# Winograd-row convolution on one core: all inputs loaded as fp32 by SyncE, cast by ScalarE, in ten planned 16-KB buffers

## The chip, the core and the metric

The kernel runs on one core of one Trainium2 chip. The metric is device time in microseconds (us). The profile is of one execution and gives times from the start of its span; TensorE is PE in it, VectorE DVE, ScalarE ACT, GpSimd POOL, SyncE SP.

## What is computed

A 3x3 convolution with padding 1, no bias: 16 images of 64 channels, 64 x 64, to 128 output channels, fp32 in and out.

```python
x_pad = np.pad(x, ((0, 0), (0, 0), (1, 1), (1, 1)), mode='constant')
output[b, co] += weight[co, ci, kh, kw] * x_pad[b, ci, kh:kh+h, kw:kw+w]   # over ci, kh, kw
```

The input is 16.8 MB, the output 33.6 MB.

## The kernel before

**Tiling.** Two images make a pair: 2 x 64 channels fill the 128 partitions, so a pair's input is one tile of 128 x 64 x 64, 16 KB per partition in fp32 (2 MB in all). There are 8 pairs. Each image of a pair has its own output tile `ot`, 128 output channels x 64 x 64 in fp32, again 16 KB per partition, 2 MB. The loop at the end runs over the pairs `p` and, in each, over four blocks `blk` of 16 output rows.

**Arithmetic.** Rows are taken two at a time. With G1 the middle row of the kernel, U is G1 applied to the sum of rows 2j and 2j+1 (tile `ss`). The even output row is U plus A, with A from G2-G1 on row 2j+1 and G0 on row 2j-1; the odd one is U plus Bt, with Bt from G0-G1 on row 2j and G2 on row 2j+2. So a block has three groups of matmuls (L165): U of 6, A of 12, Bt of 12, each over the three kernel columns and the two images, each into two PSUM tiles `acc` of 128 x 512; eight such tiles go round. ScalarE copies U to SBUF (`ut`, L179, four buffers), VectorE adds A and `ut` into the even rows of `ot` (L187) and Bt and `ut` into the odd rows (L190).

**Inputs.** Matmuls read fp16: `xs`, the pair's rows, and `ss`, the sums of rows, made by `sums` (L67) on GpSimd one pair ahead (for pair 0 on VectorE). The fp16 rows come in two ways. Pairs 0, 1 and 2 are loaded in fp32 by SyncE's queue at the start (L43, L45, L47), into buffers of the output pool, and cast to fp16 by the function `cast` (L98): pair 0's in the prologue, pair 1's by ScalarE in the last two blocks of pair 0, pair 2's by ScalarE, one piece of 16 rows in each block of pair 1. Pairs 3 to 7 are loaded by GpSimd's queue with a cast in the DMA (`load`, L58): the DMA reads fp32 from HBM and writes fp16. All five are issued early, since `xs` has eight buffers.

**Stores.** `store` (L123) writes a whole output tile of 2 MB at the end of a pair: image 0's is issued by SyncE, image 1's is put in the list `held` and issued by ScalarE in the first block of the next pair, behind the two copies to `ut`. The last pair is stored in halves of 1 MB. The output pool has seven buffers that go round.

**Order.** `keep` fixes the order of the instructions it wraps on their engine. DMA queue q1 is SyncE's, q10 ScalarE's, q0 GpSimd's; all three are worked by the same 16 DMA engines. DMAs that SyncE and ScalarE issue take their completion semaphores in turn from a set of eight; one that takes a semaphore again waits, on the issuing engine, for the DMA that had it before.

Of the kernel before, what the change touches and what calls it, by code (L numbers as in the profile page):

```python
# [8 lines left out]
F32 = mybir.dt.float32  # L9
F16 = mybir.dt.float16  # L10
# [3 lines left out]
def kernel(  # L14
# [6 lines left out]
    nc = tc.nc  # L21
    B, CI, H, W = x.shape
    CO = weight.shape[0]
    assert H == 64 and W == 64 and CI == 64 and CO == 128 and B % 2 == 0
    NP = B // 2
    RB = 8

    keep = tc.keep_in_program_order
    x_rows = x.rearrange("b c h w -> (b c) h w")
# [2 lines left out]

    const = ctx.enter_context(tc.tile_pool(name="const", bufs=1))
    psum = ctx.enter_context(tc.tile_pool(name="psum", bufs=8, space=bass.MemoryType.PSUM))
    xpool = ctx.enter_context(tc.tile_pool(name="xpool", bufs=8))
    opool = ctx.enter_context(tc.tile_pool(name="opool", bufs=7))
    spool = ctx.enter_context(tc.tile_pool(name="spool", bufs=3))
    upool = ctx.enter_context(tc.tile_pool(name="upool", bufs=4))

    w_raw = const.tile([CO, CI * 9], F32)  # L40
    nc.sync.dma_start(w_raw, w_flat)  # L41
    x0 = opool.tile([128, H, W], F32, tag="ot", name="x0")
    nc.sync.dma_start(x0, x_rows[0:128, :, :])  # L43
    x1 = opool.tile([128, H, W], F32, tag="ot", name="x1")
    nc.sync.dma_start(x1, x_rows[128:256, :, :])  # L45
    x2 = opool.tile([128, H, W], F32, tag="ot", name="x2")
    nc.sync.dma_start(x2, x_rows[256:384, :, :])  # L47
    raws = {1: x1, 2: x2}
    ident = const.tile([128, 128], F16)
    make_identity(nc, ident)  # L50
    w16 = const.tile([CO, CI * 9], F16)
    keep(nc.gpsimd.tensor_copy(w16, w_raw))  # L52

    xs = {p: xpool.tile([128, H, W], F16, tag="xs", name="xs") for p in range(3)}

    def load(p):
        xs[p] = xpool.tile([128, H, W], F16, tag="xs", name="xs")
        keep(nc.gpsimd.dma_start(xs[p], x_rows[128 * p : 128 * p + 128, :, :]))  # L58

    ss = {}  # L60

    def sums(eng, p, src, lo, n):
        if p not in ss:
            ss[p] = spool.tile([128, H // 2, W], F16, tag="ss", name="ss")
        v = src.rearrange("p (j i) c -> p j i c", i=2)
        keep(
            eng.tensor_add(  # L67
                ss[p][:, lo : lo + n, :], v[:, lo : lo + n, 0, :], v[:, lo : lo + n, 1, :]
            )
        )  # L70
# [5 lines left out]
    def wrow(i):  # L76
        return Wt[:, i, :, :].rearrange("p t c -> p (t c)")

    wps = {}
    for kh in (1, 2, 0):  # L80
# [3 lines left out]
            for q in (0, 64):  # L84
                nc.tensor.matmul(wp[q : q + 64, k * CO : k * CO + CO], w16[:, t::9], ident)  # L85
        wps[kh] = wp[:, 0 : 3 * CO]
    blank = const.tile([128, 400], F32)
    keep(nc.vector.memset(blank, 0.0))  # L88
    warm = psum.tile([128, 512], F32, tag="acc", name="warm")
    for _ in range(3):  # L90
# [3 lines left out]
    keep(nc.vector.tensor_sub(wrow(G21), wps[2], wrow(G1)))  # L94
    keep(nc.vector.tensor_sub(wrow(G01), wps[0], wrow(G1)))  # L95

    def cast(copy, p, src, lo, hi):
        keep(copy(xs[p][:, lo:hi, :], src[:, lo:hi, :]))  # L98

    for lo in (RB, 2 * RB, 3 * RB):  # L100
        sums(nc.vector, 0, x0, lo, RB)
    cast(nc.scalar.copy, 0, x0, 0, 18)
    keep(nc.scalar.copy(wrow(G0), wps[0]))  # L103
    keep(nc.scalar.copy(wrow(G2), wps[2]))
    cast(nc.gpsimd.tensor_copy, 0, x0, 34, 50)
    cast(nc.gpsimd.tensor_copy, 0, x0, 50, 64)
    for p in range(3, NP):
        load(p)
    later = {
        (0, 0): [(0, x0, 18, 34)],  # L110
        (0, 2): [(1, x1, 0, 16), (1, x1, 16, 32)],
        (0, 3): [(1, x1, 32, 48), (1, x1, 48, 64)],
    }
    later.update({(1, n): [(2, x2, 16 * n, 16 * n + 16)] for n in range(4)})

    held = []

# [2 lines left out]
    cuts_of = [(whole, whole)] * (NP - 1) + [(halves, halves)]  # L120

    def store(eng, p, b2, ot, lo, hi):
        return eng.dma_start(  # L123
            out_rows[2 * p + b2, :, lo:hi, :],
            ot.rearrange("p j i c -> p (j i) c")[:, lo:hi, :],
        )

    for p in range(NP):
        if p + 1 < NP:
            for lo in (0, 16):  # L130
                sums(nc.gpsimd, p + 1, raws.get(p + 1, xs[p + 1]), lo, 16)
        ots = [
            opool.tile([128, H // 2, 2, W], F32, tag="ot", name="ot") for _ in range(2)
        ]
        for blk in range(4):
            j0 = blk * RB

            def group(wi_rows):

                tiles = [  # L140
                    psum.tile([128, RB, W], F32, tag="acc", name="acc") for _ in range(2)
                ]
                n = 3 * len(wi_rows)
                i = 0
                for wi, off in wi_rows:
                    for kw in (1, 0, 2):
                        c_lo, c_hi = max(0, 1 - kw), min(W, W + 1 - kw)
                        for b2 in range(2):
                            p0 = 64 * b2
                            lo, hi = j0, j0 + RB  # L150
                            if off is None:
                                rhs = ss[p][p0 : p0 + 64, lo:hi, c_lo + kw - 1 : c_hi + kw - 1]
                            else:
                                while 2 * lo + off < 0:
                                    lo += 1
                                while 2 * (hi - 1) + off > H - 1:
                                    hi -= 1
                                first = 2 * lo + off
                                last = 2 * (hi - 1) + off
                                rhs = xs[p][  # L160
                                    p0 : p0 + 64,
                                    first : last + 1 : 2,
                                    c_lo + kw - 1 : c_hi + kw - 1,
                                ]
                            nc.tensor.matmul(  # L165
                                tiles[b2][:, lo - j0 : hi - j0, c_lo:c_hi],
                                Wt[p0 : p0 + 64, wi, kw, :],
                                rhs,
                                start=i == 0,
                                stop=i == n - 1,  # L170
                            )
                        i += 1
                return tiles

            U = group([(G1, None)])
            us = []
            for b2 in range(2):
                ut = upool.tile([128, RB, W], F32, tag="ut", name="ut")
                keep(nc.scalar.copy(ut, U[b2]))  # L179
                us.append(ut)  # L180
            while held:
                keep(store(nc.scalar, *held.pop(0)))
            for piece in later.get((p, blk), ()):
                cast(nc.scalar.copy, *piece)
            A = group([(G21, 1), (G0, -1)])
            for b2 in range(2):
                nc.vector.tensor_add(ots[b2][:, j0 : j0 + RB, 0, :], A[b2], us[b2])  # L187
            Bt = group([(G01, 0), (G2, 2)])
            for b2 in range(2):
                nc.vector.tensor_add(ots[b2][:, j0 : j0 + RB, 1, :], Bt[b2], us[b2])  # L190
            if blk in cuts_of[p][0]:
                store(nc.sync, p, 0, ots[0], *cuts_of[p][0][blk])
            if blk in cuts_of[p][1]:
                held.append((p, 1, ots[1], *cuts_of[p][1][blk]))
    while held:
        keep(store(nc.scalar, *held.pop(0)))

# [29 lines left out]
```

## Time and profile before

| | us |
|---|---|
| time, median of 3 runs | 126.74 (126.69 to 126.74) |
| the profiled execution's own time | 126.52 |
| its span | 124.7 |
| busy: TensorE, VectorE, ScalarE, GpSimd | 107.5, 84.6, 46.6, 37.5 |
| issue to landing: x (fp32, SyncE), xs (casting, GpSimd), 2-MB store by SyncE, by ScalarE | 12.3, 36.1, 20.4, 21.0 (medians) |

The page gives the busy time of each engine, then the span in 40 slices with the busy share in tenths, then the DMA queues, the chain of work that ended last, and the groups of instructions. A queue's line gives its packets, its MB and the time of its packets as a share of 16 engines' span. A line of the table of stretches gives the stretch and its length, then for PE, PEld (weight loads), DVE, ACT and POOL the busy us and the number of instructions, then the granted TensorE clock, the share of the DMA engines and GB/s. Bytes of a DMA are counted as they land, so a casting load counts half of what it reads; the page's HBM line counts what HBM gave and took.

### The profile page before, as it was taken

To read this page: it belongs to the slowest core of one execution; us is meant where nothing else is said; L and a number is where in the kernel's file an instruction comes from. 1 tells how busy PE (TensorE), PEld (TensorE's weight loads), DVE (VectorE), ACT (ScalarE), POOL (GpSimd) and SP (SyncE) were. 2 spreads that over 40 slices of the span, in tenths; PEclk is the share of its full clock that TensorE was granted. 3 is DMA by queue.
4 is the path that set the end of the run, shared out by engine and by line. 5 is a ranking of instruction groups with operands and counts; after the bars stand their busy time and mean duration, and the time that the engine had idled before them with its cause. 6 is when DMAs were issued, how large, how long until landed. Compare 5 with 4: busy or idle time off the path is not lost.

```text
span 124.7 us, 2423 instructions
## 1 busy us (share of the span) xinstructions
PE 107.5 (86%) x984; PEld 50.2 (40%) x984; DVE 84.6 (68%) x135; ACT 46.6 (37%) x78; POOL 37.5 (30%) x28
## 2 busy tenths in 40 slices
PE   0598999999999999999999999999999999991000
PEld 0543444444444444444444444444444444440000
DVE  1009987878877887877777778777877787775000
ACT  4108649966663332433333333333333333330000
POOL 2209992799185001920039000670000000000000
PEclk9999999999999999999999999999999999999855
DMA  5999999999999999999999999999999999999992
GB/s 145 386 436 436 431 310 260 213 168 339 381 339 365 334 381 344 357 368 347 355 360 352 355 381 413 436 436 436 415 426 431 426 426 441 426 407 413 426 418 84
DMA packets 3898, 45.52 MB, mean 365 GB/s; under 512 B 432, under 2 KB 432, under 8 KB 560
## 3 DMA queue, kind: packets, MB, share of 16 engines
q1 hardware_dynamic: 1872, 23.36, 44.9%
q10 hardware_dynamic: 1296, 16.78, 31.8%
q0 software_dynamic: 720, 5.24, 20.8%
q8 instruction: 7, 0.11, 0.3%
q14 instruction: 3, 0.02, 0.0%
HBM read 17.07 MB, written 33.55 MB: 406 GB/s over the span
## 4 chain that ended last, share of the span: by engine, by line
PE 81%; DMA 6%; DVE 2%; issue 1%; DVEq 0%; SPq 0%
PE acc L165 81%; DMA x<-in_x_dram 6%; DVE ot L187 1%; DVE ss L67 1%; DVEq L222 0%; DVE ot L190 0%; SPq L41 0%; DVEq L187 0%
## 5 line engine op out<-in xcount | busy, mean ns | idle before, releaser
L165 PE MATMUL acc<-xs,Wt 64*128 64x504 f16 (+3 forms) x768 | 87.2, 374 | 0.0
L165 PEld LDWEIGHTS <-Wt 64*128 64x128 f16 x960 | 47.4, 95 | 56.2 <-issue 1.2
L179 ACT COPY ut<-acc 128x512 f32<-128x512 f32 x64 | 34.4, 589 | 56.8 <-issue 38.1
L187 DVE TENSOR_TENSOR ot<-acc,ut 128x512 f32<-128x512 f32 x64 | 41.2, 685 | 20.7 <-PE acc L165 18.4
L190 DVE TENSOR_TENSOR ot<-acc,ut 128x512 f32<-128x512 f32 x64 | 41.1, 684 | 0.0
L67 POOL TENSOR_TENSOR ss<-xs 128x1024 f16<-128x1024 f16 x10 | 21.0, 2124 | 34.9 <-DMA xs<-in_x_dram 34.9
L165 PE MATMUL acc<-ss,Wt 64*128 64x504 f16 (+1 forms) x192 | 26.1, 377 | 0.6 <-DVE ss L67 0.6
L98 ACT CAST xs<-x 128x1024 f16<-128x1024 f32 (+1 forms) x10 | 10.5, 1068 | 3.5 <-DMA x<-in_x_dram 3.5
L67 POOL TENSOR_TENSOR ss<-x 128x1024 f16<-128x1024 f32 x4 | 9.4, 2382 | 3.2 <-DMA x<-in_x_dram 3.2
L67 DVE TENSOR_TENSOR ss<-x 128x512 f16<-128x512 f32 x4 | 3.3, 868 | 7.8 <-DMA x<-in_x_dram 7.8
L85 PE MATMUL wp<-ident,w 128*64 128x128 f16 x18 | 1.3, 328 | 4.5 <-POOL w L52 4.5
L98 POOL CAST xs<-x 128x1024 f16<-128x1024 f32 (+1 forms) x2 | 3.0, 1519 | 4.7 <-DMA x<-in_x_dram 4.7
L91 PE MATMUL warm<-blank 128*128 128x400 f32 x6 | 3.5, 738 | 0.0
L85 PEld LDWEIGHTS <-w 128*64 128x64 f16 x18 | 1.1, 209 | 4.5 <-POOL w L52 4.5
L58 POOL DMA_DIRECT2D xs<-in_x_dram x5 | 2.8, 583 | 0.0
L91 PEld LDWEIGHTS warm<-blank 128*128 128x128 f32 x6 | 1.7, 303 | 1.3 <-issue 1.0
L92 ACT CAST Wt<-wp 128x384 f16<-128x384 f32 x1 | 0.5, 478 | 3.1 <-PE wp L85 3.1
L92 ACT ACT_TABLE_LOAD x1 | 1.3, 1283 | 0.7 <-PEq L211 0.7
L52 POOL CAST w<-w_raw 128x576 f16<-128x576 f32 x1 | 0.7, 662 | 2.5 <-DMA w_raw<-in_weight_dram 2.5
L88 DVE MEMSET blank<- 128x400 f32 x1 | 0.4, 392 | 0.9 <-PEq L211 0.9
L103 ACT CAST Wt<-wp 128x384 f16<-128x384 f32 x1 | 0.5, 478 | 0.5 <-DVE Wt L95 0.5
L94 DVE TENSOR_TENSOR Wt<-wp,Wt 128x384 f16<-128x384 f32 x1 | 0.5, 549 | 0.0
(8 smaller groups left out, 1.9 us busy)
## 6 DMA issues: line engine op xcount, KB each, us to landing
out_dram<-ot SPq DMA_DIRECT2D x7, 2048.0 KB, 20.4
out_dram<-ot ACTq DMA_DIRECT2D x7, 2048.0 KB, 21.0
x<-in_x_dram SPq DMA_DIRECT2D x3, 2048.0 KB, 12.3
xs<-in_x_dram POOLq DMA_DIRECT2D x5, 1024.0 KB, 36.1
out_dram<-ot SPq DMA_DIRECT2D x2, 1024.0 KB, 10.7
out_dram<-ot ACTq DMA_DIRECT2D x2, 1024.0 KB, 11.0
w_raw<-in_weight_dram SPq DMA_DIRECT2D x1, 288.0 KB, 3.0
```

What stands on the lines that cost most here:

```text
L52: keep(nc.gpsimd.tensor_copy(w16, w_raw))
L58: keep(nc.gpsimd.dma_start(xs[p], x_rows[128 * p : 128 * p + 128, :, :]))
L67: eng.tensor_add(ss[p][:, lo : lo + n, :], v[:, lo : lo + n, 0, :], v[:, lo : lo + n, 1, :])
L85: nc.tensor.matmul(wp[q : q + 64, k * CO : k * CO + CO], w16[:, t::9], ident)
L91: nc.tensor.matmul(warm[:, 0:400], blank[:, 0:128], blank)
L92: keep(nc.scalar.copy(wrow(G1), wps[1]))
L94: keep(nc.vector.tensor_sub(wrow(G21), wps[2], wrow(G1)))
L98: keep(copy(xs[p][:, lo:hi, :], src[:, lo:hi, :]))
L165: nc.tensor.matmul(tiles[b2][:, lo - j0 : hi - j0, c_lo:c_hi], Wt[p0 : p0 + 64, wi, kw, :], rhs, start=i == 0, stop=i == n - 1,)
L179: keep(nc.scalar.copy(ut, U[b2]))
L187: nc.vector.tensor_add(ots[b2][:, j0 : j0 + RB, 0, :], A[b2], us[b2])
L190: nc.vector.tensor_add(ots[b2][:, j0 : j0 + RB, 1, :], Bt[b2], us[b2])
```

## The change

All eight pairs are loaded in fp32 by SyncE's queue. Six loads are issued at the start, ahead of any store; load 6 is issued at the end of pair 0 and load 7 at the end of pair 1, each behind that pair's first store. The casting loads on GpSimd's queue are gone. ScalarE casts pairs 2 to 7, one piece of 16 rows in each block of the pair before, as it did for pair 2. Inputs in fp32 and output tiles share ten buffers of 16 KB ("homes"), each a pool tag of its own, dealt by the lists `raw_home` and `out_home`. `xs` has three buffers instead of eight and `ss` two instead of three; `blank` is taken from the `ut` pool. The store of pair 0's second image, held for ScalarE, is issued in the third block of pair 1 instead of the first. The first stores of the pairs are wrapped in `keep`.

```diff
-    xpool = ctx.enter_context(tc.tile_pool(name="xpool", bufs=8))
-    opool = ctx.enter_context(tc.tile_pool(name="opool", bufs=7))
-    spool = ctx.enter_context(tc.tile_pool(name="spool", bufs=3))
+    xpool = ctx.enter_context(tc.tile_pool(name="xpool", bufs=3))
+    opool = ctx.enter_context(tc.tile_pool(name="opool", bufs=1))
+    spool = ctx.enter_context(tc.tile_pool(name="spool", bufs=2))
...
-    x0 = opool.tile([128, H, W], F32, tag="ot", name="x0")
-    nc.sync.dma_start(x0, x_rows[0:128, :, :])
...
+    raw_home = [0, 1, 2, 3, 4, 5, 0, 6]
+    out_home = [(6, 7), (8, 9), (1, 2), (7, 3), (8, 4), (9, 5), (1, 2), (7, 3)]
+    raws = {}
+
+    def load(p):
+        raws[p] = opool.tile([128, H, W], F32, tag=f"home{raw_home[p]}", name="raw")
+        keep(nc.sync.dma_start(raws[p], x_rows[128 * p : 128 * p + 128, :, :]))
+
+    AHEAD = 6
+    for p in range(AHEAD):
+        load(p)
+    x0 = raws[0]
...
-    def load(p):
-        xs[p] = xpool.tile([128, H, W], F16, tag="xs", name="xs")
-        keep(nc.gpsimd.dma_start(xs[p], x_rows[128 * p : 128 * p + 128, :, :]))
...
-    blank = const.tile([128, 400], F32)
+    blank = upool.tile([128, 400], F32, tag="ut", name="blank")
...
-    for p in range(3, NP):
-        load(p)
...
-    later.update({(1, n): [(2, x2, 16 * n, 16 * n + 16)] for n in range(4)})
+    later.update({(p, n): [(p + 1, *q4[n])] for p in range(1, NP - 1) for n in range(4)})
...
-                sums(nc.gpsimd, p + 1, raws.get(p + 1, xs[p + 1]), lo, 16)
+                sums(nc.gpsimd, p + 1, raws[p + 1], lo, 16)
         ots = [
-            opool.tile([128, H // 2, 2, W], F32, tag="ot", name="ot") for _ in range(2)
+            opool.tile([128, H // 2, 2, W], F32, tag=f"home{k}", name="ot")
+            for k in out_home[p]
         ]
...
-            while held:
+            while held and (p, blk) not in ((1, 0), (1, 1)):
                 keep(store(nc.scalar, *held.pop(0)))
...
-                store(nc.sync, p, 0, ots[0], *cuts_of[p][0][blk])
+                keep(store(nc.sync, p, 0, ots[0], *cuts_of[p][0][blk]))
             if blk in cuts_of[p][1]:
                 held.append((p, 1, ots[1], *cuts_of[p][1][blk]))
+            if blk == 3 and p + AHEAD < NP:
+                load(p + AHEAD)
```

More of the change, by code (lines that the diff above doesn't have):

```diff
@@ L41 @@
     nc.sync.dma_start(w_raw, w_flat)
-    x0 = opool.tile([128, H, W], F32, tag="ot", name="x0")
-    nc.sync.dma_start(x0, x_rows[0:128, :, :])
[L44 to L48, printed above, removed]
+    raw_home = [0, 1, 2, 3, 4, 5, 0, 6]
[8 more added lines that the diff above has]
+    x0 = raws[0]
     ident = const.tile([128, 128], F16)
@@ L52 @@
     keep(nc.gpsimd.tensor_copy(w16, w_raw))
-    xs = {p: xpool.tile([128, H, W], F16, tag="xs", name="xs") for p in range(3)}
-    def load(p):
-        xs[p] = xpool.tile([128, H, W], F16, tag="xs", name="xs")
-        keep(nc.gpsimd.dma_start(xs[p], x_rows[128 * p : 128 * p + 128, :, :]))
+    xs = {}
     ss = {}
@@ L95, with cast @@
     keep(nc.vector.tensor_sub(wrow(G01), wps[0], wrow(G1)))
-    def cast(copy, p, src, lo, hi):
-        keep(copy(xs[p][:, lo:hi, :], src[:, lo:hi, :]))
+    def cast(copy, p, lo, hi):
+        if p not in xs:
+            xs[p] = xpool.tile([128, H, W], F16, tag="xs", name="xs")
+        keep(copy(xs[p][:, lo:hi, :], raws[p][:, lo:hi, :]))
     for lo in (RB, 2 * RB, 3 * RB):
         sums(nc.vector, 0, x0, lo, RB)
-    cast(nc.scalar.copy, 0, x0, 0, 18)
+    cast(nc.scalar.copy, 0, 0, 18)
     keep(nc.scalar.copy(wrow(G0), wps[0]))
     keep(nc.scalar.copy(wrow(G2), wps[2]))
-    cast(nc.gpsimd.tensor_copy, 0, x0, 34, 50)
-    cast(nc.gpsimd.tensor_copy, 0, x0, 50, 64)
-    for p in range(3, NP):
-        load(p)
+    cast(nc.gpsimd.tensor_copy, 0, 34, 50)
+    cast(nc.gpsimd.tensor_copy, 0, 50, 64)
+    q4 = [(16 * n, 16 * n + 16) for n in range(4)]
     later = {
-        (0, 0): [(0, x0, 18, 34)],
-        (0, 2): [(1, x1, 0, 16), (1, x1, 16, 32)],
-        (0, 3): [(1, x1, 32, 48), (1, x1, 48, 64)],
+        (0, 0): [(0, 18, 34)],
+        (0, 2): [(1, *q4[0]), (1, *q4[1])],
+        (0, 3): [(1, *q4[2]), (1, *q4[3])],
     }
-    later.update({(1, n): [(2, x2, 16 * n, 16 * n + 16)] for n in range(4)})
+    later.update({(p, n): [(p + 1, *q4[n])] for p in range(1, NP - 1) for n in range(4)})
     held = []
```

## The prediction, made before the changed kernel ran

> **What bounds the kernel now.** I read the page first: the slices, the queues and the chain.
>
> ```profile
> PE   0598999999999999999999999999999999991000
> DMA  5999999999999999999999999999999999999992
> ...
> q1 hardware_dynamic: 1872, 23.36, 44.9%
> q10 hardware_dynamic: 1296, 16.78, 31.8%
> q0 software_dynamic: 720, 5.24, 20.8%
> ...
> HBM read 17.07 MB, written 33.55 MB: 406 GB/s over the span
> ...
> PE 81%; DMA 6%; DVE 2%; issue 1%; DVEq 0%; SPq 0%
> ```
>
> Two rows of slices are full at once. TensorE runs from 9.82 us to 112 without a gap, and the chain names it at 81%. The chain, however, ends with VectorE's last add at 114.0; the span ends at 124.7. The missing 10.7 us are the landing of the last stores, so the DMA row decides: it is full from slice 1 to slice 38. The queue shares add to 97.5% of 16 engines' time. The bytes that HBM sees are 17.07 + 33.55 = 50.62 MB; the page's 45.52 MB counts q0's casting loads by what lands, fp16, half of what they read.
>
> Next the table of stretches, to see what rate the saturated engines reach with and without casting loads (last columns: DMA share, GB/s as landed).
>
> ```profile
> 4.00:15.00 11.00, 9.90 (x72) 5.25 (x74) 5.93 (x10) 5.42 (x9) 6.32 (x9) 1.00 1.00 427
> ...
> 20.00:26.00 6.00, 6.00 (x61) 2.83 (x58) 4.68 (x8) 5.32 (x8) 3.28 (x2) 1.00 1.06 216
> 26.00:29.00 3.00, 3.00 (x32) 1.35 (x30) 2.27 (x5) 2.02 (x3) 3.00 (x2) 1.00 0.97 183
> ...
> 78.00:114.00 36.00, 34.59 (x324) 15.79 (x320) 28.27 (x46) 11.81 (x22) 4.21 (x2) 1.00 1.00 426
> ```
>
> The fp32 loads alone (4 to 15) move 427 GB/s, the stores alone (78 to 114) 426. The casting loads alone (20 to 26) land 216, so they read 432: a casting load costs the same engine time as an fp32 load of the same source. Only 26 to 29 is poorer: its queue answer has q0 0.32 MB landed (0.64 read), q1 0.18, q10 0.05, in all 0.87 MB where 3.0 x 0.427 = 1.28 would fit. That is 0.41 MB, 0.96 us of saturated engines lost at full share.
>
> Last, the DMA view of the end, 114 to 124.7 in 40 slices of 0.27 us.
>
> ```profile
> DMA  9989999999899999999989999997465530000000
> GB/s 459 398 367 398 429 429 429 459 490 398 337 459 429 398 429 490 429 398 398 429 368 459 459 429 459 398 429 306 184 276 245 245 153 31 0 0 0 0 0 0
> ```
>
> The rate holds to 121.2, then falls off until 123.1: some engines finish 2 us before others. The remainder, (306+184+276+245+245+153+31) x 0.27 us = 0.39 MB, is 0.9 us for all sixteen, so an even finish would come at 122.1. Unevenness costs 1.0 us, and 1.6 us more follow to the end of the span.
>
> **The change, part by part.** The profiled execution took 126.52 us, 1.8 beyond its span; the median of the runs is 126.74, 0.22 above it. Differences of the span are applied to the median. A measurement here can tell about 0.2%, 0.25 us, from no change.
>
> *Bytes.* Five casting loads become five fp32 loads. HBM bytes stay 50.62 MB; engine time per load stays (432 against 427). What can go is the loss of 26 to 29: between 0 (it comes back in another place) and -0.96. I take -0.96: no fp32 load and no store in the four stretches shows such a loss. Check from below: 0 to 4 us moved 188 x 4 = 0.75 MB and stays; (50.62 + 0.14 of instruction queues - 0.75) / 0.427 = 117.1 us, so an even finish at 121.1 instead of 122.1. Same 1.0 us.
>
> *The uneven finish.* It grew either in the casting queue or in the stores; bounds 0 and -1.0, and I take the middle, -0.5, as no view separates the engines.
>
> The Trainium skill, DMA: Bandwidth & Descriptors, section Latency and other measured facts, says that engines 7 and 15 are usually slower, as a best guess because the descriptor rings of GpSimd's loads share their ports, and that loads issued by SyncE or ScalarE don't have such rings. By that rule the whole 1.0 would go and the sum would be -2.0; the trace shows the uneven finish, not its cause.
>
> *ScalarE.* 20 casts of 128x1024 more at 1.06 us: 46.6 + 21.2 = 67.8 us. In each of the pairs 2 to 6 it does 8 x 0.589 + 4 x 1.06 = 8.95 us of 12.8. Before has such a pair already: in pair 1 (22.5 to 35.2) ScalarE is busy 9.01 us and TensorE has no gap, 12.50 of 12.50 between 22.5 and 35. Cost 0. Behind a cast stand the next block's copies to ut; they have a slack of one block, 3.2 us, since the PSUM tile waited for is the fourth group back. If the cover went, each 1 us of lateness over that would stop TensorE 1 us.
>
> *GpSimd.* Five DMA issues of 0.58 go. Ten sums read fp32, 2382 instead of 2124 ns: +2.6 us, 4.8 us per pair of 12.8. With two ss buffers the sums for pair p+1 wait until TensorE has done the last U group of pair p-1, about 2.5 us before pair p starts; they then end early in pair p. Nothing is queued behind them that is due. Cost 0.
>
> *SyncE.* x0 stays the first after the weights, so the start (9.07 us) stays. At 4.9 us per 2.1 MB, x5 lands at 9.05 + 5 x 4.9 = 33.6. Behind it in q1 come pair 0's store (its data ready at 23.7), load 6, pair 1's store, load 7, pair 2's store. The new wait: load 7 goes to home 6 and so stands on SyncE until pair 0's store has landed; behind it stands pair 2's store, ready at 49.4. From 33.6 q1 and q10 share: the answer for 76 to 112 gives them 50.6% and 49.5%, so 213 GB/s or 9.8 us per 2.1 MB each. Pair 0's store lands by 43.4, 6 us before pair 2's store needs SyncE. Cost 0.
>
> *ScalarE's stores.* Pair 0's second store is held from 24.4 to about 31 (third block of pair 1) and shares from 33.6: landed by about 43.4. Home 7 is written next by pair 3, VectorE at 50.5. Cost 0, cover 7 us.
>
> *Home 8* is the tight one. Pair 1's first store, third in q1, lands at 33.6 + 3 x 9.8 = 63.0 if q10 always takes its half, or up to 4 us earlier where q10 comes in late. VectorE's first add of pair 4 into it starts at 63.43 in before. TensorE needs that add's PSUM banks only at the last group of the second block, at 66.3; an add of two halves takes 1.3, so TensorE stops only if the landing is later than 65.0. Cost 0, cover 2 us. The later homes have more: pair 2's first store, two places on in q1, lands by about 80 and is needed at 89.
>
> *blank* in the ut pool is read for the last time before the blocks start. Cost 0.
>
> Sum: -0.96 - 0.5 = -1.5. Span 123.2, median 125.2. How far could it go? The chain of TensorE stays, and its last store is issued at 113.99. The weights' load of 288 KB took 3.0 us to land, 0.7 of it bytes, so 2.3 fixed; the last two 1-MB stores take 4.9; from the last landing (113.99 + 9.7) to the span's end is 1.0: 113.99 + 2.3 + 4.9 + 1.0 = 122.2. So at most -2.5, 124.2.
>
> **The rivals.**
>
> *Little or no gain, 126.2 to 126.7.* The casting loads already read at the full rate. If 26 to 29 is the price of the first stores starting against deep queued loads (they were issued at 23.75 and 24.35), it returns at about 33, and with the unevenness unchanged nothing is left. For: these stores come just ahead of the loss. Against: in 15 to 20 a second queue starts beside a first with no such loss (328 landed, half of it casting). Chance 0.22. The Trainium skill, same page, section Bandwidth, says that HBM binds at about 358 GB/s for a core's transfers to and from HBM; by it bytes to HBM alone count and the change brings nothing. The trace disagrees: 427 in three stretches.
>
> *More gain, 124.2 to 124.5.* All engines finish together, and the floor of 122.2 that TensorE's last store sets decides, plus the 2.04 between span and median. Chance 0.10.
>
> *Slower, about 129.4.* Home 8 comes late. If q10 takes more than its half, q1's three transfers stretch. That happens in the trace: in 108 to 114 q10 has 62.1% and q1 35.9%, though there q1 carries packets of half the size. At 40% of 427, 171 GB/s, pair 1's store lands at 33.6 + 6.29/0.171 = 70.4; TensorE stops 70.4 - 65.0 = 5.4 us, its floor moves to 122.2 + 5.4 = 127.6, time 129.4 to 129.6. It costs anything only from a landing at 66.0 on, and makes the kernel slower from 67.5 on, a share under 43.5%. Against: all packets here are 16 KB, and 76 to 112 shares evenly. With other waits of the ten homes, chance 0.10.
>
> **How the numbers follow.** Forecast (0.8 to 2.2 us gained, 124.5 to 125.9) 0.58; little or nothing 0.22; floor 0.10; slower 0.10. The range 124.2 to 126.6 holds the forecast, the floor and most of the second case: 0.86. Faster by over 0.25 us: 0.58 + 0.10 + 0.13 of the second case = 0.81; same 0.08; slower 0.10 and a hundredth for small losses, 0.11.
>
> **What would show it.** Right: no q0; DMA row full from slice 1 to the end at 425 to 430 GB/s with no stretch like 26 to 29; TensorE without gap from 9.8 to 111.4; last store issued at 114.0 and landing about 1.5 us earlier; ScalarE near 68 us. Wrong: TensorE gaps at pair 4 released by VectorE, VectorE waiting on a DMA out of ot (home 8); a DMA row under 9 between 33 and 114, which would mean that the stores run dry; or a new poor stretch near 33.

## The result, and the profile after

The changed kernel takes 128.12 us (median of 4 runs, 127.80 to 128.19) against 126.74: ratio 1.0100, 95% interval 1.0080 to 1.0119. It is slower by 1.0%; forecast was 125.2, a gain of 1.5 us. The profiled execution took 128.16 us, its span is 126.4, so 1.7 us over that of before (124.7).

The page of the changed kernel: the rows of slices, the queues and the chain.

```profile
PE   0689999999999999999999999999999999970000
...
DMA  5899999999899999999999999999999999999960
GB/s 161 363 441 446 425 420 420 430 451 394 332 430 430 438 425 420 428 430 441 425 410 430 425 446 430 415 425 425 436 441 415 425 410 420 449 392 420 438 254 10
...
q1 hardware_dynamic: 2592, 33.85, 64.1%
q10 hardware_dynamic: 1296, 16.78, 31.2%
...
HBM read 17.07 MB, written 33.55 MB: 401 GB/s over the span
...
PE 79%; DMA 6%; DVE 2%; issue 1%; DVEq 0%; ACT 0%; SPq 0%; ACTq 0%
```

q0 is gone, the bytes are the same, and TensorE works through as before. Two things differ from the forecast. Slices 9 and 10 (28 to 35 us) fall to 394 and 332 GB/s: a new poor stretch. And the row ends worse: the last two slices hold 254 and 10 GB/s. The table of stretches prices the first (last column GB/s):

```profile
18.00:29.00 11.00, 11.00 (x106) 5.07 (x104) 8.63 (x14) 8.96 (x13) 5.10 (x3) 1.00 1.01 432
29.00:30.00 1.00, 1.00 (x14) 0.41 (x11) 1.00 (x3) 0.20 (x1) 0.00 (x0) 1.00 0.84 360
30.00:34.00 4.00, 4.00 (x40) 1.85 (x38) 2.92 (x5) 2.77 (x5) 0.86 (x1) 1.00 1.01 348
...
78.00:114.00 36.00, 35.03 (x328) 18.38 (x323) 28.26 (x46) 18.50 (x29) 4.69 (x2) 1.00 1.00 425
```

From 29 to 34 us (427 - 360) x 1 + (427 - 348) x 4 = 383 KB are missing, 0.90 us of saturated engines. Before lost 0.41 MB, 0.96 us, from 26 to 29. The loss came back some 4 us later, at the same price.

The DMA view of the end, 114 to 126.4 in 40 slices of 0.31 us, prices the second:

```profile
DMA  9999999999999999999999975543110000000000
GB/s 449 396 423 423 423 423 423 423 423 423 423 423 423 423 423 423 423 423 423 423 423 423 423 317 238 211 211 132 53 53 26 26 26 26 0 0 0 0 0 0
```

The rate holds to 121.1 (121.2 before). What is left, (317+238+211+211+132+53+53+4x26) x 0.31 = 0.41 MB, would take all sixteen engines 0.96 us: an even finish at 122.1, exactly as before. But the tail at 53 and 26 GB/s, one or two engines' worth, runs to 124.5 instead of 123.1. The landings in the trace say it once more. They show the last store in 16 parts, which I take to be one for each engine: the middle one (the ninth) landed at 122.7 (123.0 before) and the last at 125.32, 2.6 us behind it (before 123.70, 0.7 behind). The fifteenth landed at 123.72; before, the sixteenth landed at 123.70. So fifteen parts are in by the time at which all were in before, and one is late: 1.6 of the 1.7 us.

### The profile page after: what moved, and what is told of

It is laid out like the page before. It is cut to its first block, busy times and chain, and to the rows that moved or that the text cites. A ratio compares the mean times of both kernels' runs of the same rounds, so it can differ in the third digit from the quotient of the medians.

```text
span 126.4 us, 2450 instructions
## 1 busy us (share of the span) xinstructions
PE 107.9 (85%) x984; PEld 53.1 (42%) x984; DVE 84.2 (67%) x135; ACT 65.8 (52%) x98; POOL 37.2 (29%) x23
## 4 chain that ended last, share of the span: by engine, by line
PE 79%; DMA 6%; DVE 2%; issue 1%; DVEq 0%; ACT 0%; SPq 0%; ACTq 0%
PE acc L170 79%; DMA raw<-in_x_dram 6%; DVE ot L192 1%; DVE ss L70 1%; DVE ot L195 0%; DVEq L229 0%; ACT ut L184 0%; SPq L41 0%; DVEq L192 0%; ACTq L184 0%
## 5 line engine op out<-in xcount | busy, mean ns | idle before, releaser
L170 PE MATMUL acc<-xs,Wt 64*128 64x504 f16 (+3 forms) x768 | 90.3, 373 | 0.2 <-DVE ot L192 0.2
L170 PEld LDWEIGHTS <-Wt 64*128 64x128 f16 x960 | 50.4, 94 | 53.9 <-issue 1.9
L70 POOL TENSOR_TENSOR ss<-raw 128x1024 f16<-128x1024 f32 x14 | 32.8, 2364 | 45.1 <-issue 33.2
L103 ACT CAST xs<-raw 128x1024 f16<-128x1024 f32 (+1 forms) x30 | 31.6, 1060 | 3.4 <-DMA raw<-in_x_dram 3.3
L170 PE MATMUL acc<-ss,Wt 64*128 64x504 f16 (+1 forms) x192 | 28.7, 377 | 0.6 <-DVE ss L70 0.6
L70 DVE TENSOR_TENSOR ss<-raw 128x512 f16<-128x512 f32 x4 | 3.3, 866 | 7.5 <-DMA raw<-in_x_dram 7.5
L103 POOL CAST xs<-raw 128x1024 f16<-128x1024 f32 (+1 forms) x2 | 3.0, 1518 | 4.6 <-DMA raw<-in_x_dram 4.6
L95 ACT CAST Wt<-wp 128x384 f16<-128x384 f32 x1 | 0.5, 479 | 3.0 <-PE wp L88 3.0
L108 ACT CAST Wt<-wp 128x384 f16<-128x384 f32 x1 | 0.5, 479 | 0.5 <-DVE Wt L98 0.5
L97 DVE TENSOR_TENSOR Wt<-wp,Wt 128x384 f16<-128x384 f32 x1 | 0.6, 550 | 0.0
L98 DVE TENSOR_TENSOR Wt<-wp,Wt 128x384 f16<-128x384 f32 x1 | 0.5, 548 | 0.0
L109 ACT CAST Wt<-wp 128x384 f16<-128x384 f32 x1 | 0.5, 485 | 0.0
```

Source lines behind the costliest of these rows:

```text
L70: eng.tensor_add(ss[p][:, lo : lo + n, :], v[:, lo : lo + n, 0, :], v[:, lo : lo + n, 1, :])
L95: keep(nc.scalar.copy(wrow(G1), wps[1]))
L103: keep(copy(xs[p][:, lo:hi, :], raws[p][:, lo:hi, :]))
L170: nc.tensor.matmul(tiles[b2][:, lo - j0 : hi - j0, c_lo:c_hi], Wt[p0 : p0 + 64, wi, kw, :], rhs, start=i == 0, stop=i == n - 1,)
```

## The experiments

Theory A at first was that the poor stretch is the start of ScalarE's queue. What stood in the end is theory G: one DMA engine is some 6% slow on stores while no casting load runs. (Some expectations limit it to 16-KB packets; f2 below refutes that limit.) Its measure is a count in the trace: of the 16-KB packets on q1 and q10 that start between 36 and 110 us, those that take 20 to 100 ns more than the usual 611. Here it is, with the sum of their excess over 611, and by how much the last part of the store issued last lands behind its middle part:

| kernel | slow packets | their excess, us | last landing behind the middle, us | ratio to before |
|---|---|---|---|---|
| before | 59 | 2.1 | 0.7 | 1 |
| after | 100 | 3.7 | 2.6 | 1.0100 |
| after, all in one queue (s1) | 96 | 3.5 | 2.8 | 1.0118 |
| after, five loads fp32 by GpSimd (g1) | 89 | 3.2 | 2.7 | 1.0115 |
| after, home 8 exchanged (e1) | 96 | 3.5 | 2.4 | 1.0087 |
| after, two casting loads (k1) | 69 | 2.6 | 1.4 | 1.0014 |
| before, longer casting (d2) | 29 | 1.1 | 0.8 | 0.9976 |
| after, no hold (n1) | 97 | 3.5 | 2.3 | 1.0122 |
| after, early small load (a1) | 112 | 4.0 | 2.6 | 1.0125 |
| before, early small load (b1) | 55 | 2.0 | 1.3 | 1.0000 |
| before, early small store (b3) | 57 | 2.1 | 0.8 | 0.9993 |

In e1 and n1 the store issued just ahead of the last one lands last of all, 3.3 and 3.2 us behind its own middle part. b1 shows how far the landings of a single profile can be trusted: 1.3 against the 0.7 of before, at the same time.

That they are one engine's is read from three things. In a stretch of 6 us with stores alone mostly 9 or 10 of about 157 packets are slow, which is a sixteenth. One part of the last stores is late by more than the rest. And the slow packets form a chain: s1, where all data goes through one queue, has 27 of them between 82.5 and 100 us, and each starts within 5 ns of the end of the one before it. In before, 44 of the 47 between 76 and 106 us start at the end of another slow one; the chain begins at 74.1 us, as the last casting loads end, and the packet ahead of it in the chain took 611 ns.

### Where the poor stretch comes from: a1, b1, b3, n1

a1 and b1 put a small DMA on ScalarE's queue at the start, in the changed kernel and in the one before:

```diff
     nc.sync.dma_start(w_raw, w_flat)
+    touch = const.tile([CO, 16], F32)
+    keep(nc.scalar.dma_start(touch, w_flat[:, 0:16]))
```

> The changed kernel, plus one small load (64 bytes a partition, into a tile nobody reads) that ScalarE issues at about 1 us, so that its first DMA isn't the held store at 29.92. Theory A (the poor stretch of 30.5 to 33.5 us follows ScalarE's first DMA, as that of 26 to 28.5 in the kernel before followed its first at 24.35): no poor stretch near 31, end about 0.9 us earlier, 127.2. Rival B (it belongs to the first stores, whoever issues them): the stretch stays, 128.1. If the finish is set by one lagging DMA engine alone, that engine still loses its 1.4 us at 19 to 24 us, and the last landing stays 2 to 3 us behind the median either way.

> The kernel before, plus the same small early load by ScalarE. Theory A: the poor stretch of 26 to 28.5 us goes, 125.8. Rival B: 126.7.

Measured: 128.25 (ratio 1.0125, 1.0110 to 1.0140) and 126.71 (1.0000, 0.9988 to 1.0011). The stretch of a1:

```profile
26.00:29.00 3.00, 3.00 (x30) 1.37 (x28) 2.27 (x4) 2.02 (x3) 0.00 (x0) 1.00 1.00 426
29.00:30.00 1.00, 1.00 (x14) 0.46 (x10) 1.00 (x3) 0.27 (x1) 0.00 (x0) 1.00 0.89 377
30.00:34.00 4.00, 4.00 (x40) 1.78 (x38) 2.85 (x5) 2.78 (x6) 0.94 (x1) 1.00 1.01 344
```

344 GB/s at 30 to 34, though ScalarE's queue had been used (b1: 186 at 26 to 29, where before had 183): theory A falls. b3 puts an early write of 64 bytes per partition in front instead, in the kernel before:

```diff
+    early = const.tile([CO, 16], F32)
+    keep(nc.vector.memset(early, 0.0))
+    keep(nc.scalar.dma_start(out_rows[0, :, 0, 0:16], early))
```

> The kernel before plus one early store of 64 bytes a partition (zeros, into output that pair 0's store overwrites) issued by ScalarE at about 1 us. Theory B (the poor stretch of 25.5 to 28.5 us belongs to the first write to the output, whoever issues it): the stretch goes, 125.8. Rival I (it belongs to the first big stores, their size or place, not to being first): 126.7 with the stretch where it was.

Measured 126.55 (0.9993, 0.9968 to 1.0017), and 26 to 29 is as poor as ever (191 GB/s landed, 183 before): not the first write as such. n1 moves the first 2-MB store without moving the loads, by dropping the hold in the changed kernel:

```diff
-            while held and (p, blk) not in ((1, 0), (1, 1)):
+            while held:
```

> The changed kernel without the hold: pair 0's second store is issued by ScalarE in the first block of pair 1 (about 24.4 us) instead of the third (about 31), while SyncE's loads go on to 33.6. Theory I (the poor stretch of about 3 us belongs to the first big store, whenever it starts): the stretch moves to about 25 to 28.5 us, none is at 30 to 33.5. Rival (it belongs to the end of the first run of loads, 23.9 in the kernel before and 33.6 in the changed one): it stays at 30 to 33.5. Under both the bytes lost are about 0.4 MB and the uneven finish stays, so the time is 127.9 to 128.4; if the stretch vanishes, 127.2.

Measured 128.22 (1.0122, 1.0097 to 1.0147). Its stretches:

```profile
24.00:26.00 2.00, 2.00 (x22) 0.93 (x20) 1.40 (x4) 1.48 (x2) 0.92 (x1) 1.00 1.11 451
26.00:28.00 2.00, 2.00 (x22) 0.88 (x18) 1.27 (x3) 1.47 (x3) 0.00 (x0) 1.00 1.02 270
28.00:30.00 2.00, 2.00 (x22) 0.92 (x20) 2.00 (x4) 0.79 (x2) 0.00 (x0) 1.00 0.91 385
30.00:34.00 4.00, 4.00 (x40) 1.81 (x38) 2.88 (x5) 2.77 (x6) 0.91 (x1) 1.00 0.96 406
```

The hole has moved to 26 to 30, and costs the same: (427 - 270) x 2 + (427 - 385) x 2 = 0.40 MB. It goes with the first big store, not with the end of the loads. Two runs shown below for another reason agree: in s1, where ScalarE issues no DMA at all, it is at 30 to 34 us (311 GB/s), and in g1, where SyncE's first store has no loads queued ahead of it, at 26 to 29 (279 GB/s), although ScalarE's first store is held there until 30. So it does not matter which engine issues the store. In the packets it is the *loads* that are slow: in about the 2 us ahead of the store's first packet (28.4 here, 33.2 in the changed kernel, 27.6 in before) some 30 to 40 packets take over 700 ns, half of them 850 to 1210, where a 16-KB packet otherwise takes 611 and a casting one 624. Why a first big store does this to loads in flight was not found.

### Home 8 and the bytes: e1, h1

The changed kernel did have the wait that the third rival named. Its waits, in VectorE's lines and SyncE's (total us, times, longest):

```profile
DVE ot L192 <- DMA out_dram<-ot: 2.9, 1, 2.9
...
SPq L50 <- DMA out_dram<-ot: 9.8, 1, 9.8
```

The last part of pair 1's first store landed at 65.07, 2.1 later than the 63.0 predicted (its middle part at 63.87), and TensorE stopped: its records have a gap of 0.22 us. e1 exchanges homes 8 and 9 for pairs 4 and 5:

```diff
-    out_home = [(6, 7), (8, 9), (1, 2), (7, 3), (8, 4), (9, 5), (1, 2), (7, 3)]
+    out_home = [(6, 7), (8, 9), (1, 2), (7, 3), (9, 4), (8, 5), (1, 2), (7, 3)]
```

> The changed kernel with homes 8 and 9 swapped between pairs 4 and 5, so that pair 4 writes where pair 1's second store was (landed at 56.2), and VectorE's wait of 2.9 us for pair 1's first store at pair 4 has nothing to wait for. If the end is set by the slow DMA engine: 128.1, no change, although the wait is gone. If the 0.5 us that TensorE lost there count: 127.6.

Measured 128.00 (1.0087, 1.0068 to 1.0107): VectorE's wait is gone, the last store is issued 0.49 us earlier (113.75 against 114.24), and the interval holds the ratio of the changed kernel itself, 1.0100. The wait lay beside the bound and cost nothing that can be measured. h1 leaves out loads 6 and 7 (pairs 6 and 7 use pair 0's input), so 4.2 MB less is moved:

```diff
-                load(p + AHEAD)
+                raws[p + AHEAD] = raws[0]
```

> The changed kernel without loads 6 and 7: pairs 6 and 7 use pair 0's input, so 4.2 MB of 50.6 are left out, 9.8 us of all engines' work. If the end is set by the DMA engines' total work and by the slow one's lag, the engines now run dry before the end, the lag is made up, and the end falls to what TensorE's last stores need: 113.99 + 8.2, span 122.2, time 124.2. If something else of the change (homes, ScalarE's casts, waits) holds the end up: above 126.

Measured 125.05 (0.9864, 0.9840 to 0.9887), span 123.2:

```profile
DMA  4999999999999999999989965996399819999992
```

Now the DMA engines run dry (6, 5, 6, 3, 1) and the end is set by TensorE's last store. That is the floor which the prediction had put at a span of 122.2 and a time of 124.2; the span is 1.0 higher, since from the issue of the last store (113.84) to the end it took 9.4 us and not the 8.2 of the prediction. Its count of slow packets is not comparable: whole groups of some 15 packets that start together are slow in it too. 4.2 MB would take 9.8 us; the gain is 3.1, so the bound of the changed kernel is the DMA engines, with about 3 us to that floor.

### Queue, cast, or neither: s1, g1, k1, d2

s1 issues the second stores by SyncE too, so that all data goes through one queue:

```diff
-                held.append((p, 1, ots[1], *cuts_of[p][1][blk]))
+                keep(store(nc.sync, p, 1, ots[1], *cuts_of[p][1][blk]))
```

> The changed kernel with all stores issued by SyncE, so that q1 carries everything and ScalarE issues no DMA. Theory A: no poor stretch near 31. For the uneven finish, theory C (single engines lose time to transfers of their own, instruction fetches above all, and nothing hands their work on): the last landing is still 2 to 3 us behind the median; with A the time is about 127.0. Rival D (two queues on the same engines drift apart and make the finish uneven): finish even, 125.2 to 125.6. Home 8 should not be waited for: pair 1's first store is fourth in q1 after the loads, landing at about 33.6 + 4 x 4.9 = 53.

Measured 128.24 (1.0118, 1.0094 to 1.0141). One queue does not change the loss, so it isn't the sharing of queues. With one queue the order is plain: of the 2-MB stores that land from 85 to 101 us, the last part is 1.9, 2.1, 2.4 and 2.7 us behind the middle one, 0.2 to 0.3 more each time. The engine carries 8 packets of a store, and 8 packets that are slow by 36 ns make 0.29 us.

g1 gives loads 3 to 7 back to GpSimd's queue, but in fp32, with ScalarE's casts as in the changed kernel:

```diff
-    def load(p):
+    def load(p, eng=nc.gpsimd):
...
-        keep(nc.sync.dma_start(raws[p], x_rows[128 * p : 128 * p + 128, :, :]))
+        keep(eng.dma_start(raws[p], x_rows[128 * p : 128 * p + 128, :, :]))
...
-    for p in range(AHEAD):
-        load(p)
+    for p in range(3):
+        load(p, nc.sync)
...
+    for p in range(3, AHEAD):
+        load(p)
...
+        if p in (1, 3):
+            load({1: 6, 3: 7}[p])
...
-            if blk == 3 and p + AHEAD < NP:
-                load(p + AHEAD)
```

> The changed kernel, but loads 3 to 7 are issued by GpSimd's queue, still in fp32 and still cast by ScalarE: 3 to 5 where the casting loads were issued, load 6 ahead of the sums in pair 1, load 7 ahead of those in pair 3. So three queues share the engines as in the kernel before, and only the cast in the DMA is gone. If the casting itself cost time: 125.2 to 126.2. If the casting loads cost nothing and the loss of the change lies in putting all loads into SyncE's queue ahead of the stores: 126.7, like before. If it lies in the ten homes or ScalarE's casts: 128.

Measured 128.16 (1.0115, 1.0098 to 1.0131). GpSimd's queue alone brings nothing back; 3 to 7 slow packets per 6 us are there while its fp32 loads run (34 to 70 us), of about 104 (a sixteenth is 6.5). k1 instead makes loads 6 and 7 casting again, issued at 50.7 and 74.7 us (the first sooner than the 61 expected):

```diff
-    later.update({(p, n): [(p + 1, *q4[n])] for p in range(1, NP - 1) for n in range(4)})
+    later.update({(p, n): [(p + 1, *q4[n])] for p in range(1, 5) for n in range(4)})
...
+        if p in (4, 5):
+            xs[p + 2] = xpool.tile([128, H, W], F16, tag="xs", name="xs")
+            raws[p + 2] = xs[p + 2]
+            keep(nc.gpsimd.dma_start(xs[p + 2], x_rows[128 * (p + 2) : 128 * (p + 2) + 128, :, :]))
...
-            if blk == 3 and p + AHEAD < NP:
-                load(p + AHEAD)
```

> The changed kernel, but loads 6 and 7 are casting loads by GpSimd's queue again, issued late (at the starts of pairs 4 and 5, when an xs buffer comes free, about 61 and 74 us); the six loads ahead, the ten homes and ScalarE's other casts stay. Theory G: one DMA engine writes to HBM 6% slower (about 650 instead of 611 ns for a 16-KB store packet), and it falls behind whenever its packets are stores and fp32 loads; a casting packet reads 16 KB but writes 8, which gives its write side the time to keep up. So the engine should stop falling behind from 61 to about 90 us, some 46 packets x 38 ns = 1.7 us: time 126.3 to 126.7, no slow store packets in that stretch. Rival H (casting has nothing to do with it; the loss is in the order of the transfers or in the homes): 128.1.

Measured 126.98 (1.0014, 1.0000 to 1.0027): 1.1 of the 1.4 us are back. Between 58 and 70 and between 82 and 94, where casting loads are in the mix, no packet of about 110 in 6 us is slow; in between there are 9 and 4, and after it 8 to 11. From 58 to 70 us g1 has fp32 loads on the same queue, and 10 of 204 packets are slow there: the cast makes the difference, not the place of the loads. The end of k1, 114 to 125.1 in slices of 0.28 us, has a shorter tail:

```profile
GB/s 443 384 472 443 443 413 443 443 413 354 443 472 384 472 413 443 443 443 413 413 384 443 384 472 384 354 325 295 266 118 30 59 59 59 0 0 0 0 0 0
```

d2 goes the other way from the kernel before: its casting loads of pairs 6 and 7 are cut into halves of 32 rows, smaller packets that take a smaller share, so that casting lasts to 94 us instead of 76:

```diff
-        keep(nc.gpsimd.dma_start(xs[p], x_rows[128 * p : 128 * p + 128, :, :]))
+        for lo, hi in ((0, 32), (32, 64)) if p >= 6 else ((0, 64),):
+            keep(nc.gpsimd.dma_start(xs[p][:, lo:hi, :], x_rows[128 * p : 128 * p + 128, lo:hi, :]))
```

> The kernel before with the casting loads of pairs 6 and 7 each issued as two halves of 32 rows, so that a packet reads 8 KB and its queue takes 1/5 instead of 1/3 of the bytes beside two store queues: the same loads last until about 92 us instead of 77. Theory G: the slow engine keeps up for 15 us more, about 26 packets x 38 ns = 1.0 us, and no longer ends behind the next ones: 125.9 to 126.4. Rival H: 126.7.

Measured 126.41 in 10 runs (0.9976, 0.9964 to 0.9987), the fastest of all that compute the whole output. Until 94 us at most 2 packets in 6 us are slow, and 9 from there on. The gain is small, since by then other engines are as late as the slow one (its last landing is 0.8 us behind the middle, as in before).

### Stores in parts: t1, t1c, t2, f1, f2, f3

Three kernels were to find the slow engine by giving the last partitions of one store to a DMA of their own, pair 6's first store as 120 + 8 partitions (t1 from the changed kernel, t2 from the one before) or 112 + 16 (t1c):

```diff
+        flat = ot.rearrange("p j i c -> p (j i) c")
+        if (p, b2) == (6, 0):
+            keep(eng.dma_start(out_rows[2 * p + b2, 0:120, lo:hi, :], flat[0:120, lo:hi, :]))
+            return eng.dma_start(out_rows[2 * p + b2, 120:128, lo:hi, :], flat[120:128, lo:hi, :])
```

> The changed kernel with one store split by partitions: pair 6's first store (2 MB) goes as 120 partitions and then 8. A DMA of 120 partitions spreads 8 each over fifteen engines and leaves the sixteenth free of eight 16-KB packets, 4.9 us of its work. The traces so far: from the end of the loads on (about 34 us in the changed kernel, 76 in the one before) about ten store packets in every 6 us take 640 to 660 ns instead of 611, as many as one engine carries, and none do while casting loads run. Theory E (that one engine, slower by 6% at stores, sets the end, and it is the last of the sixteen): the last landing comes 1.5 to 2.5 us earlier, time 126.0 to 126.8. Rival F (the lag has another cause, or it is another engine): 128.1 or a little more.

> Control for the split: the same store as 112 and 16 partitions, which load all sixteen engines alike (7 and 1 packets). Theory E and rival F both: 128.1, no change; if it gains as t1_skip16th does, the split itself helps and not the freed engine.

> The kernel before with the same 120 + 8 split of pair 6's first store. Its slow engine ends 0.7 us behind the group of the next ones, so theory E: 0.5 to 0.9 us gained, 125.8 to 126.2. Rival F: 126.7.

Measured 133.02 (1.0485), 130.07 (1.0273) and 132.80 (1.0463). All missed. The stretches of t1 say why:

```profile
96.00:102.00 6.00, 6.00 (x60) 3.12 (x58) 4.76 (x8) 3.55 (x6) 0.00 (x0) 1.00 1.06 423
102.00:112.00 10.00, 10.00 (x96) 5.24 (x94) 7.73 (x13) 3.22 (x6) 0.00 (x0) 1.00 0.96 271
```

While a store of 120 partitions is in work the rate falls from 423 to 271 GB/s (t2 296; with 112 partitions 356), many packets taking over 1000 ns. In t1 that is 152 GB/s for 10 us, 1.5 MB or 3.6 us of all engines, which hides any gain from a freed engine; which engine is slow stays open. Why the split costs so much was not found either.

f1, f2 and f3 store in halves of 32 rows, so in packets of 8 KB: the changed kernel, the one before, and d2.

```diff
-    cuts_of = [(whole, whole)] * (NP - 1) + [(halves, halves)]
+    cuts_of = [(halves, halves)] * NP
```

> The changed kernel with every store in two halves of 32 rows (1 MB, packets of 8 KB instead of 16 KB), the first half issued two blocks earlier; loads as before. Theory G (one DMA engine is slow on store packets of 16 KB only, about 100 packets of 640 to 660 ns instead of 611 between 36 and 110 us, and this is what makes its last store land 2.6 us behind the others): 8-KB store packets show no such excess, so the last landing is under 1.2 us behind the median one and the time is 126.3 to 126.9. Rival (the engine is slow in bytes written, whatever the packet, or the loss comes from HBM): 128.1, the last landing again 2.5 us behind. Rival (the smaller DMAs cost more each, or take a semaphore of eight again too soon and hold ScalarE up): over 128.5, with TensorE gaps released by ScalarE.

> The kernel before with every store in halves (8-KB packets). Theory G: its 59 slow packets (2.1 us in excess over 611 ns between 36 and 110 us) go, but its last landing is only 0.7 us behind the median, so 125.9 to 126.5. Rival (bytes written): 126.7. Rival (smaller DMAs cost more): over 127.

> The kernel before with the casting loads of pairs 6 and 7 in halves (which alone gave 126.41) and every store in halves as well. Theory G: nothing more than either alone, since both take the same slow packets away: 125.9 to 126.4. Rival (the two gains are of different causes): the two add up, under 125.9.

Measured 133.36 (1.0522, 1.0462 to 1.0583), 127.84 (1.0075, 1.0059 to 1.0091) and 127.52 (1.0050, 1.0033 to 1.0066). The claim that 8-KB packets escape falls: in f2 from 70 to 112 us, with no casting, 12 to 17 of about 311 packets in 6 us take 318 to 355 ns against 309, again near a sixteenth (19). The slowness goes with the stores, whatever the packet. f2 and f3 are slower than their whole-store versions by 1.0 and 1.1 us. An 8-KB packet takes 309 ns, not half of 611, and by that the 256 of them on each engine would cost 0.9 us. That this is the whole reason is not shown: in f2 the last part also lands 1.7 us behind the middle one.

f1 lost its time to another thing, the last rival of its expectation. A store that ScalarE issues stood until load 6, issued at 24.0, had landed at 54.9, and behind it stood the copies to `ut`. From the waits of f1, and its stretches:

```profile
PE acc L170 <- ACT ut L184: 7.9, 1, 7.9
...
46.00:50.00 4.00, 3.02 (x30) 1.28 (x27) 0.54 (x1) 0.00 (x0) 3.97 (x2) 1.00 1.02 426
50.00:57.00 7.00, 0.09 (x1) 0.09 (x1) 0.11 (x1) 1.67 (x3) 0.69 (x1) 0.65 1.00 421
57.00:60.00 3.00, 3.00 (x15) 1.17 (x16) 2.70 (x5) 2.48 (x5) 0.00 (x0) 0.50 1.08 459
```

With twice as many stores, SyncE and ScalarE come round their eight semaphores in half the time and meet a load that is still queued: TensorE stands for 7.9 us. So f1 says nothing on the finish of the changed kernel; f2 and f3 do.

## Why the prediction was wrong

**The bound was right.** DMA engines bind both kernels, casting loads and fp32 loads cost the same engine time, and an even finish is at 122.1 in both. The step "HBM bytes stay, engine time per load stays" holds.

**The first term, -0.96 us, was wrong.** The step that failed is "no fp32 load and no store in the four stretches shows such a loss". The stretch belongs to the first big store and returned at 29 to 34 us, 0.90 us. The rival of little or no gain had named this ("it returns at about 33"), with the stores just ahead of the loss as its evidence; the start of a second queue at 15 to 20, which was held against it, is not the same event, since the second queue there carried loads. n1 shows it, by moving the store alone. The prediction had listed a new poor stretch near 33 among its signs of being wrong, and it came.

**The second term, -0.5 us, had the wrong sign; it is what made the kernel slower.** It was bounded by 0 and -1.0, on the thought that an uneven finish can only shrink when one of its two possible sources is removed. It grew: the last landing went from 0.7 to 2.6 us behind the middle one, +1.6 us at the end. The casting loads were not a source of unevenness, but what kept one engine's stores from being slow. The excess of slow packets grew from 2.1 to 3.7 us, by 1.6 as well. That the two agree to a tenth is luck: in g1 the excess is 1.1 us above before, and the last landing 1.7 later. That the cast matters, and neither the queue nor the amount of data, rests on g1 against k1 (same queue, fp32 no gain, casting 1.1 us back) and on the stretches of before, k1 and d2, in which slow packets are nearly absent as long as casting loads run. How a casting load does it was not found. The slow packets of a casting stretch are others: about half of all take 624 ns instead of 611, 2% on many engines in place of 6% on one.

The Trainium skill, DMA: Bandwidth & Descriptors, section Latency and other measured facts, expects slower engines and guesses at the descriptor rings of GpSimd's loads. The trace agrees that an engine is slow (about 650 against 611 ns), but not with the guess: s1 and the changed kernel issue no DMA from GpSimd and have the most of it, and casting loads by GpSimd take it away. The -2.0 by that rule missed by 3.4 us.

**The rival on the slower side** had the sign, by another mechanism. Home 8 did come late, at 65.07 against the 65.0 from which it was said to decide, and VectorE waited 2.9 us, until 65.41; the working had left out these 0.3 us between the landing and the add. e1 took the wait away and left the time. The price of 5.4 us needed a share for q10 of 60%; from 33.6 to 65 us it was 47.2%.

**The steps at no cost held.** ScalarE was busy 65.8 us (67.8 forecast) and TensorE lost nothing to it; load 7 stood 9.8 us on SyncE for home 6 with nothing urgent behind it, as worked out; the last store by ScalarE was issued at 114.24, 0.25 later than before.

The range was too narrow on the side of a loss: its upper end, 126.6, came from the rival of little or no gain, and no bound of the unknown term reached above nothing, though no view had separated the engines.

## What to carry to other kernels

Where the DMA engines bind, the end is set by the slowest one of sixteen: read how far the last part of the last store lands behind the middle one, and let an unknown effect on that evenness have both signs. A loss seen beside two events (here casting loads and a first store) must not be credited to the one that the change removes, until a run moves one without the other. Cutting DMAs to another number of partitions or into smaller packets can cost more than an uneven finish: 2.7 to 4.8% and 0.8% here.

## What the runs showed of the hardware

- One DMA engine takes about 650 ns for a 16-KB store packet where the others take 611. While casting loads run it hardly does (k1: 0 of 215 packets from 58 to 70 us), and on loads it doesn't (after: 0 of 629 packets from 4 to 28 us). In 8-KB packets it is about 330 against 309 (f2).
- While casting loads run, about half of all 16-KB store packets take 624 ns instead of 611 (before, 34 to 74 us: 47%).
- For about 2 us ahead of the first packets of the first 2-MB store, 30 to 40 packets of the loads in flight take over 700 ns, half of them 850 to 1210, instead of 611. It cost 0.90 us in the changed kernel, 0.96 in before and 0.40 MB, or 0.94, in n1.
- A 2-MB store of 120 partitions brings the sixteen engines from 423 to 271 GB/s while it is in work, one of 112 to 356.
- After TensorE had stood 7.9 us (f1), the granted clock was 0.50 from 57 to 60 us.
